# Low-rank tiles 5.2 apart instead of 4.4, their three products in another order, and the last block inversion spread over 32 instead of 25

## The chip, the cores and the metric

The kernel runs on one core of one Trainium2 chip. The metric is the device time of one execution in microseconds, and of several executions the median. The engines are named as in the profile: PE multiplies matrices (PEld is its loading of the stationary operand), DVE, ACT and POOL work elementwise, SP issues most of the DMAs.

## The reference, cut to what matters

Two layers on 512 positions of width 2048. Layer 0 is forgetting attention, layer 1 is RWKV-7 time mixing; each is a gated branch with a residual add. The change lies in layer 1:

```python
xx = jnp.pad(h[:, :-1], ((0, 0), (1, 0), (0, 0))) - h
xr, xw, xk, xv, xa, xg = (h + xx * mu[i] for i in range(6))
r, k, v, z = xr @ w_in[0], xk @ w_in[1], xv @ w_in[2], xg @ w_in[3]
w_log = -softplus(-(w0 + tanh(xw @ w1) @ w2)) - 0.5
v = v + (v_first - v) * sigmoid(v0 + (xv @ v1) @ v2)
a = sigmoid(a0 + (xa @ a1) @ a2)
# per head, over 512 steps: S = S * w_t + (S a_t) b_t + v_t k_t ; y_t = S r_t
```

The first factors of the low-rank pairs, w1 (96 columns), a1 (96) and v1 (64), are the *low-rank stage* here. The recurrence is done in chunks of 64 steps, and each chunk needs the inverse of a unit triangular 64x64 matrix per head; the 32x32 diagonal blocks of four 128-row tiles (eight heads) are inverted together, so there are four *block inversions*.

## The kernel before, in words

Positions lie along the free axis (512), the width in 16 tiles of 128 partitions. A product of full precision is made of three matmuls of rounded halves: high by high, low by high, high by low (`mm3`). The *backbone* is the chain of the large projections: 16 output tiles per weight, each of 16 input tiles, so 48 matmuls into a bank named `pj`. In layer 1 it goes through 10 tiles of k, then 16 each of r, v, z and the output. Its weights come by SP (`raw`), are rounded by ACT (`whi`), and DVE makes the rest (`wlo`), once for every four input tiles, that is once for 12 `pj` matmuls.

All else runs beside the backbone as tasks. A planner (`Flow`) keeps a clock that only the issued matmuls advance: a matmul of 512 columns counts 0.213. A task yields numbers, each the time on that clock after which it goes on. PE, DVE and ACT take their instructions strictly in the order in which the planner issued them, so a changed number changes these orders, from its place to the end of the program.

- `lora_k(q, k)` is the low-rank stage for input tile k. It loads the hidden tile (`hp`) and the weights (`rawl`); POOL makes the difference `d` to the position before; DVE makes three mixed operands `m` (for w, a and v, in this order); ACT rounds each (`mh`); the rests (`ml`) are made by POOL for w and by DVE for a and v; DVE also makes the rest of the weights, `wll`. Then three products, each three matmuls, go into banks: w and a into two named `S`, v into `y`. `side` starts one such tile every 4.4.
- `keys` prepares the operands of four 128-row tiles and then starts `invert` for them. A block inversion is 30 steps of two operations on `lane` and `lt`, by POOL for the first three groups and by DVE for the last (`DG = (3,)`), with a yield after each step. `inverse` takes the result further with small matmuls (`x<-t,gab` and `x<-qt,us`), started for the last group at `DINV + 8`:

```python
e = dve if grp in DG else pool
e.tensor_tensor(out=t, in0=m[:, 0:s, s:s + 1]..., in1=m[:, s:s + 1, s + 1:]..., op=OP.mult)
e.tensor_tensor(out=m[:, 0:s, s + 1:], in0=m[:, 0:s, s + 1:], in1=t, op=OP.add)
if grp in DG:
    yield DINV / 30
```

- `mixing` brings the 16 input tiles of the next projection: loads (`hp`), `hi` by ACT, `lo` by DVE or POOL, in a burst at the end of the projection before. `values` finishes v (loads `sv` and `vf`, three DVE operations per tile). The recurrence (`recur`) starts when all inverses are there and ends before the output projection begins.

Of the kernel before, what the change touches and what calls it, by code (L numbers as in the profile page):

```python
# [131 lines left out]
def body(ctx, tc, a, out, dbg=None, stop=0):  # L132
# [26 lines left out]
    def bank(tag, bufs=None):  # L159
        return cur["p"].tile([P, T], F, tag=tag, bufs=cur["t"][tag], name=tag)  # L160
# [71 lines left out]
    def act_hi(hi, src):  # L232
        act.activation(hi, src, AF.Copy)
# [19 lines left out]
    def mm3(o, w, k, x, first, last, m0=0, m1=P):  # L253
        wh, wl = w
        xh, xl = x
        pe.matmul(o, wh[:, k, m0:m1], xh, start=first, stop=False)
        pe.matmul(o, wl[:, k, m0:m1], xh, start=False, stop=False)
        pe.matmul(o, wh[:, k, m0:m1], xl, start=False, stop=last)
# [30 lines left out]
    def silu_c(mp):  # L289
        cb = mp.tile([P, D], F, name="cb", bufs=1)  # L290
        cs = mp.tile([P, KT], F, name="cs", bufs=1)
        i = act.activation(cs, vecs[:, V_C], AF.Silu)
        return cb, cs, i
# [17 lines left out]
    def load(q, src, tag, shape=(P, T), bufs=None):  # L311
        t = q.tile(list(shape), F, tag=tag, name=tag, bufs=bufs)
        sp.dma_start(t, src)
        return t
# [81 lines left out]
    with ExitStack() as s0:  # L396
# [7 lines left out]
        with tc.tile_pool(name="st0", bufs=2, reuse_waits="tile") as q:  # L404
# [97 lines left out]
            cb, cs, i = silu_c(cbp)  # L502
# [11 lines left out]
            for i in range(4):  # L514
                o = bank("tr")
# [619 lines left out]
    def keep(j, o):  # L1135
        t = mq.tile([P, T], F, tag="z", name="kt")
        act.activation(t, o, AF.Copy)
        yield 1.5
        sp.dma_start(kTd[j], t)


    lspan = ((0, LW), (LW, LW + LA_), (NL - P, NL))
    lb, la = [], []

    def lora_k(q, k):
        if k == 0:
            lb.extend(bank(t) for t in "SSy")
        hp = load(mq, h1d[k], "hp", (P, T + 1), bufs=NHP)
        raw = load(q, a["lora"][k], "rawl", (P, NL))
        yield 4  # L1150
        wh = q.tile([P, 1, NL], R, tag="whl", name="whl")
        wl = q.tile([P, 1, NL], R, tag="wll", name="wll")
        act_hi(wh[:, 0], raw)
        ns = (1, 4, 3)
        ms = [q.tile([P, T], F, tag=f"m{n}", name="m", bufs=1 + (n == 3)) for n in ns]
        d = q.tile([P, T], F, tag="d", name="d")
        pool.tensor_tensor(out=d, in0=hp[:, 0:T], in1=hp[:, 1:], op=OP.subtract)
        ts = [tuple(q.tile([P, T], R, tag=f"m{x}{n}", name="m" + x) for x in "hl") for n in ns]
        yield 1.4
        for i in range(5):  # L1160
            if i == 1:
                dve.tensor_tensor(out=wl[:, 0], in0=raw, in1=wh[:, 0], op=OP.subtract)
            if i < 3:
                dve.scalar_tensor_tensor(out=ms[i], in0=d,
                                         scalar=vecs[:, V_MU + ns[i], k:k + 1],
                                         in1=hp[:, 1:], op0=OP.mult, op1=OP.add)
            if 1 <= i < 4:
                act_hi(ts[i - 1][0], ms[i - 1])
            if 2 <= i:
                e = pool if i - 2 < 1 else dve  # L1170
                e.tensor_tensor(out=ts[i - 2][1], in0=ms[i - 2], in1=ts[i - 2][0],
                                op=OP.subtract)
            yield 0.7
        yield 1
        sp.dma_start(mxd[0, k], ms[2])
        premixed.add((0, k))
        for t, o, (m0, m1) in zip(ts, lb, lspan):
            mm3(o[0:m1 - m0, :], (wh, wl), 0, t, k == 0, k == KT - 1, m0, m1)
            yield 1
        if k == KT - 1:  # L1180
            lb.append(None)

    def lora_act(q):
        for o, (m0, m1), fn, nm in zip(lb, lspan, (AF.Tanh, AF.Copy), "wa"):
            t = q.tile([m1 - m0, T], F, tag="t", name="t", bufs=1)
            act.activation(t, o[0:m1 - m0], fn)
            h = q.tile([m1 - m0, T], R, tag=nm + "h", name=nm + "h", bufs=1)
            l = q.tile([m1 - m0, T], R, tag=nm + "l", name=nm + "l", bufs=1)
            split(h, l, t)
            la.append((h, l))  # L1190
        t = q.tile([2 * LV, T], F, tag="t", name="t", bufs=1)
        o = lb[2][P - LV:]
        for i in range(2):
            act.activation(t[i * LV:i * LV + LV], o, AF.Copy)
        h = q.tile([2 * LV, T], R, tag="vh", name="vh", bufs=1)
        l = q.tile([2 * LV, T], R, tag="vl", name="vl", bufs=1)
        pool.memset(l[LV:].bitcast(F), 0.0)
        act_hi(h, t)
        dve.tensor_tensor(out=l[0:LV], in0=t[0:LV], in1=h[0:LV], op=OP.subtract)
        la.append((h, l))  # L1200
# [3 lines left out]
    def lora_w(q, g, n):  # L1204
        nm, rows = (("w2", LW), ("a2", LA_), ("v2", LV))[n]
        raw = load(q, a[nm][:, g * T:(g + 1) * T], "w2r", (rows, T), bufs=3)
        if n == 2:
            wh = q.tile([2 * LV, T], R, tag="v2h", name="v2h", bufs=2)
        else:
            wh = q.tile([rows, T], R, tag="w2h", name="w2h", bufs=4)  # L1210
            wl = q.tile([rows, T], R, tag="w2l", name="w2l", bufs=4)
        yield 6.5
        act_hi(wh[0:rows], raw)
        yield 1.2
        if n == 2:
            dve.tensor_tensor(out=wh[LV:], in0=raw, in1=wh[0:LV], op=OP.subtract)
        else:
            dve.tensor_tensor(out=wl, in0=raw, in1=wh, op=OP.subtract)
        yield 1.2
        uw[g, n] = (wh,) if n == 2 else (wh, wl)  # L1220
# [529 lines left out]


    STW = 5
    DG, DINV = (3,), 25
    HOP = 3.9
    INV, KEY = 54, 9.8

    def side(q):
        for j, o in enumerate(ks):
            fl.start(0, keep(j, o))
        for k in range(KT):  # L1760
            fl.start(fl.t, lora_k(q, k))
            yield 4.4
        while len(lb) < 4:
            yield 0.2
        yield 0.5
        pools.close()
        q = pools.enter_context(tc.tile_pool(name="uq", bufs=2, reuse_waits="tile"))
        for n in range(3):
            fl.start(fl.t, lora_w(q, 0, n))
        rmask = q.tile([P, NCH, C], F, name="rmask", bufs=1)  # L1770
        pool.memset(rmask, 1.0)
        pool.memset(rmask[:, :, 0:1], 0.0)
        rms.append(rmask)
        lora_act(q)
        yield 3.5
        for j in range(KT):
            for n in range(3):
                if j % 4 == 0 and j < KT - 4:
                    fl.start(fl.t, lora_w(q, j // 4 + 1, n))
                fl.start(fl.t, lora_up(q, j, n))  # L1780
                yield 0.8
        while len(ups) < 3 * KT:
            yield 0.2
        yield 3
        pools.close()
        kp = pools.enter_context(tc.tile_pool(name="kp", bufs=1, reuse_waits="tile"))
        eIs.append(kp.tile([P, NCH, C + 1], F, name="eI"))
        for i in range(5):
            qts.append(kp.tile([P, NCH, C], F, name=f"qt{i}"))
            for r in (32, 96):  # L1790
                pool.memset(qts[i][r:r + 32, :, 0:32], 0.0)
        pool.memset(eIs[0][:, :, 0:1], 1.0)
        for j in range(KT):
            if "v" in dbg:
                print("keys", j, fl.t, len(ends))
            fl.start(fl.t, keys(kp, j))
            fl.start(fl.t + 5, mixz(kp, j))
            yield KEY
        while len(qd) < KT or len(premixed) < 3 * KT:
            yield 0.2  # L1800
        yield 3
        pools.close()
        rk = pools.enter_context(tc.tile_pool(name="rk", bufs=1, reuse_waits="tile"))
        for i in range(4):
            QP.append([rk.tile([P, NJ, C], F, name=f"QP{i}{h}") for h in range(2)])
            GP.append([rk.tile([P, NJ, C], F, name=f"GP{i}{h}") for h in range(2)])
            for h in range(2):
                pool.memset(QP[i][h][OS[h]], 0.0)
                pool.memset(GP[i][h][OS[h]], 0.0)
        def stages():  # L1810
            for n in range(NG * NU):
                g, u = divmod(n, NU)
                while any(NJ * g + i not in rd for i in range(NJ)):
                    yield 0.2
                yield from stage(rk, g, u)

        fl.start(fl.t, stages())
        fl.start(fl.t, recur(rk))

    fl.start(0, side(q))  # L1820
    Av, Ar, Az, G = [], [], [], []
    ready = {(id(A), k) for k in range(KT)}
# [37 lines left out]
```

## Time and profile before

| what | us |
|---|---|
| runs of the kernel before | 2422.9, 2425.7, 2427.42; median 2425.7 |
| profiled execution, its own time | 2421.53 |
| its span, first to last instruction | 2419.5 |
| PE busy in the span | 2307.1 |
| PE not busy in the span | 112.4 |

The rows below come from the profiled execution; microseconds count from the start of its span. All rows have the line of one helper (L90), so the names of the tiles tell the place. The granted clock is given as a share of 2.4 GHz.

### The profile page before, as it was taken

Reading aid. Unit: us, or ns where it says so; the run is one execution under the profiler, and the core shown is the slowest. Engines: PE = TensorE matmul, PEld = TensorE weight load, DVE = VectorE, ACT = ScalarE, POOL = GpSimd, SP = SyncE. Lnnn points to the kernel's source line nnn. Section 1 sums busy time; section 2 is a strip of 40 time slices with the busy share of each in tenths; the row PEclk is TensorE's granted clock in tenths of the full one; section 3 lists DMA queues with packets and bytes.
Section 4 is the critical chain, followed back from the end, with each engine's and each line's share of the span. In section 5 each row is a group of like instructions: output and inputs, shape, how many; then the busy total and the mean of one; then the engine's idle time right before and its main releaser. Section 6 shows DMA issues by size and latency. Waiting matters only on the chain. (4 is left out here: it accounts for less than half of the span.)

```text
span 2419.5 us, 39366 instructions
## 1 busy us (share of the span) xinstructions
PE 2307.1 (95%) x13626; PEld 1804.9 (75%) x13626; DVE 1611.3 (67%) x2850; ACT 1254.4 (52%) x2298; POOL 699.6 (29%) x1114
## 2 busy tenths in 40 slices
PE   6999899999999999998999999889899989999999
PEld 4787677877777778886766767667677767777887
DVE  6886678788888645336797667666577777655322
ACT  3436655555555544225646777754345556665221
POOL 0003333434333110110141209851264545440000
PEclk8999999999999999999999999999999999999999
DMA  8864366666666365445756999877776766645543
GB/s 310 323 226 157 112 202 210 216 215 221 209 220 207 123 199 189 144 135 153 224 168 212 296 282 274 262 213 200 217 198 180 200 183 192 179 121 173 160 138 96
DMA packets 388151, 480.22 MB, mean 198 GB/s; under 512 B 146032, under 2 KB 217840, under 8 KB 384112
## 3 DMA queue, kind: packets, MB, share of 16 engines
q1 hardware_dynamic: 386288, 475.08, 63.3%
q0 software_dynamic: 1664, 2.63, 0.3%
q8 instruction: 108, 1.77, 0.3%
q14 instruction: 91, 0.75, 0.1%
HBM read 381.63 MB, written 95.95 MB: 197 GB/s over the span
## 5 line engine op out<-in xcount | busy, mean ns | idle before, releaser
L90 PE MATMUL pj<-hi,whi 128*128 128x512 f32 x2416 | 985.7, 408 | 14.6 <-ACT hi L90 8.2
L90 PE MATMUL pj<-hi,wlo 128*128 128x512 f32 x2416 | 958.0, 397 | 6.1 <-DVE wlo L90 6.1
L90 PE MATMUL pj<-lo,whi 128*128 128x512 f32 x2416 | 958.7, 397 | 0.0
L90 DVE TENSOR_TENSOR wlo<-raw,whi 128x512 fp32r<-128x512 f32 (+2 forms) x628 | 477.8, 768 | 278.5 <-ACT whi L90 275.2
L90 ACT ACTIVATE whi<-raw 128x512 fp32r<-128x512 f32 (+2 forms) x628 | 394.1, 634 | 423.7 <-PE pj L90 221.2
L90 PEld LDWEIGHTS pj<-hi,whi 128*128 128x128 f32 x2416 | 458.7, 190 | 119.7 <-ACT hi L90 9.0
L90 PEld LDWEIGHTS pj<-lo,whi 128*128 128x128 f32 x2416 | 457.4, 189 | 108.7 <-DVE lo L90 0.2
L90 PEld LDWEIGHTS pj<-hi,wlo 128*128 128x128 f32 x2416 | 459.0, 190 | 100.0 <-DVE wlo L90 7.4
L90 DVE CUSTOM_DVE_ANT_0 wm<-wm,cb 128x1024 f32<-128x1024 f32 x128 | 156.6, 1224 | 0.3
L90 POOL TENSOR_SCALAR SV<-SV,dec 64x64 f32<-64x64 f32 x224 | 98.8, 463 | 108.6 <-DVE SV L90 71.6
L90 ACT ACTIVATE pr<-Sm,mx 128x128 f32<-128x128 f32 (+3 forms) x128 | 71.5, 558 | 85.5 <-POOL mx L90 81.5
L90 POOL TENSOR_SCALAR mx<-mx 128x1 f32<-128x1 f32 x128 | 65.6, 513 | 154.9 <-DVE mx L90 117.9
L90 POOL TENSOR_SCALAR pr<-pr,rc 128x128 f32<-128x128 f32 (+3 forms) x128 | 87.6, 685 | 33.0 <-DVE rc L90 29.6
L90 DVE CUSTOM_DVE_ANT_0 Sm<-S,cmask 128x128 f32<-128x128 f32 (+3 forms) x128 | 62.0, 485 | 36.0 <-PE S L90 35.4
L90 POOL TENSOR_TENSOR lt<-lane 128x30 f32<-128x30 f32 (+14 forms) x90 | 63.2, 702 | 64.0 <-DMA lane<-mld 57.1
L90 POOL TENSOR_TENSOR lane<-lane,lt 128x30 f32<-128x30 f32 (+14 forms) x90 | 65.6, 729 | 7.1
L90 POOL TENSOR_TENSOR bk<-bk,eI 128x512 f32<-128x512 f32 x32 | 36.5, 1140 | 105.0 <-PE S L90 59.6
L90 PE MATMUL S<-k,q 128*128 128x128 f32 (+7 forms) x256 | 62.6, 327 | 0.0
L90 POOL TENSOR_TENSOR acc<-acc,sq 128x512 f32<-128x512 f32 x14 | 18.1, 1295 | 150.8 <-ACT sq L90 150.8
L90 PE MATMUL tr<-ident,pr 128*128 128x128 f32 x320 | 57.3, 277 | 4.3 <-DVE pT L90 1.4
L90 PEld LDWEIGHTS tr<-ident,pr 128*128 128x128 f32 x320 | 41.6, 141 | 25.4 <-ACT pT L90 6.9
L90 DVE SCALAR_TENSOR_TENSOR hp<-pj,gate,hp 128x512 f32<-128x512 f32 x16 | 12.0, 751 | 68.9 <-PE pj L90 68.9
(325 smaller groups left out, 3282.4 us busy)
## 6 DMA issues: line engine op xcount, KB each, us to landing
wm<-in_wmodT SPq DMA_DIRECT2D x132, 512.0 KB, 4.4
raw<-in_wz SPq DMA_DIRECT2D x128, 256.0 KB, 3.8
raw<-in_wo SPq DMA_DIRECT2D x128, 256.0 KB, 3.5
raw<-in_wv SPq DMA_DIRECT2D x124, 256.0 KB, 3.9
wm<-in_wmodT SPq DMA_DIRECT2D x30, 1024.0 KB, 6.8
raw<-in_wk SPq DMA_DIRECT2D x96, 256.0 KB, 3.7
raw<-in_wr SPq DMA_DIRECT2D x64, 256.0 KB, 4.8
raw<-in_wq SPq DMA_DIRECT2D x56, 256.0 KB, 3.6
```

The costliest lines, as they stand in the source:

```text
L90: self.last = f(*a, **k)
```

## The change

The start of the next low-rank tile is 5.2 of the planner's clock away, not 4.4. The three products of a tile are issued as a, v, w instead of w, a, v, so that the one whose rest comes from POOL is last. The last block inversion spreads its 30 steps over 32 of the clock, not 25; as its `inverse` tasks start at `DINV + 8`, they are 7 later too.

```diff
-        for t, o, (m0, m1) in zip(ts, lb, lspan):
+        for t, o, (m0, m1) in ((ts[i], lb[i], lspan[i]) for i in (1, 2, 0)):
             mm3(o[0:m1 - m0, :], (wh, wl), 0, t, k == 0, k == KT - 1, m0, m1)
             yield 1
...
-    DG, DINV = (3,), 25
+    DG, DINV = (3,), 32
...
         for k in range(KT):
             fl.start(fl.t, lora_k(q, k))
-            yield 4.4
+            yield 5.2
```

On PE, in the low-rank stage, one tile before: its rows (`S_11402` is the bank of w, `S_11403` of a, `y` of v; `ml` is the rest that DVE or POOL made) stand like this, and the next tile's w follows after 6 or 9 more `pj` rows.

```order
L90 MATMUL S_11402<-mh_11747,whl_11739 96x512
L90 MATMUL S_11402<-mh_11747,wll_11740 96x512
L90 MATMUL S_11402<-ml_11748,whl_11739 96x512
L90 MATMUL pj_11733<-hi_10939,whi_11652 128x512
L90 MATMUL pj_11733<-hi_10939,wlo_11653 128x512
L90 MATMUL pj_11733<-lo_10940,whi_11652 128x512
L90 MATMUL S_11403<-mh_11749,whl_11739 96x512
L90 MATMUL S_11403<-mh_11749,wll_11740 96x512
L90 MATMUL S_11403<-ml_11750,whl_11739 96x512
```

On PE at the same place in the changed program: a comes first (its last row stands on top here), then v, then w, and the next tile's a follows after 9 or 15 `pj` rows.

```order
L90 MATMUL S_11403<-ml_11781,whl_11770 96x512
L90 MATMUL pj_11699<-hi_11233,whi_11725 128x512
L90 MATMUL pj_11699<-hi_11233,wlo_11726 128x512
L90 MATMUL pj_11699<-lo_11234,whi_11725 128x512
L90 MATMUL y_11404<-mh_11782,whl_11770 128x512
L90 MATMUL y_11404<-mh_11782,wll_11771 128x512
L90 MATMUL y_11404<-ml_11783,whl_11770 128x512
L90 MATMUL pj_11699<-hi_11275,whi_11725 128x512
L90 MATMUL pj_11699<-hi_11275,wlo_11726 128x512
L90 MATMUL pj_11699<-lo_11276,whi_11725 128x512
L90 MATMUL S_11402<-mh_11778,whl_11770 96x512
```

From the first tile's first product to the last tile's, 201 `pj` rows stood before and 261 stand now; the stage's own matmuls are the same, and everything on PE behind the stage comes 57 `pj` rows later against the backbone (the first matmul of the recurrence 48, its last 57).

On DVE, in the last block inversion, before (steps of two rows on `lane` and `lt`; `wlo` belongs to the backbone):

```order
L90 TENSOR_TENSOR wlo<-raw,whi 128x512
L90 TENSOR_TENSOR lt<-lane 128x130
L90 TENSOR_TENSOR lane<-lane,lt 128x5x26
L90 TENSOR_TENSOR lt<-lane 128x150
L90 TENSOR_TENSOR lane<-lane,lt 128x6x25
L90 TENSOR_TENSOR lt<-lane 128x168
L90 TENSOR_TENSOR lane<-lane,lt 128x7x24
L90 TENSOR_TENSOR wlo<-raw,whi 128x512
```

And the same steps on DVE in the changed program (`lo<-hp,hi` belongs to the mixing burst):

```order
L90 TENSOR_TENSOR wlo<-raw,whi 128x512
L90 TENSOR_TENSOR lt<-lane 128x130
L90 TENSOR_TENSOR lane<-lane,lt 128x5x26
L90 TENSOR_TENSOR lt<-lane 128x150
L90 TENSOR_TENSOR lane<-lane,lt 128x6x25
L90 TENSOR_TENSOR lo<-hp,hi 128x512
L90 TENSOR_TENSOR wlo<-raw,whi 128x512
L90 TENSOR_TENSOR lt<-lane 128x168
L90 TENSOR_TENSOR lane<-lane,lt 128x7x24
L90 TENSOR_TENSOR wlo<-raw,whi 128x512
```

Between the first and the last row of the inversion stood 10 `wlo`, 5 `lo` and 4 transposes of `inverse`; now 12, 8 and 4.

## Rows read from the trace of the kernel before

**Rows 1.** Page, part 1: busy time, share of the span, instructions of each engine.

```profile
PE 2307.1 (95%) x13626; PEld 1804.9 (75%) x13626; DVE 1611.3 (67%) x2850; ACT 1254.4 (52%) x2298; POOL 699.6 (29%) x1114
```

**Rows 2.** Windows: a dense stretch, low-rank stage, last inversion, recurrence, stretch behind it.

```profile
core 0: us, PE busy (x) PEld busy (x) DVE busy (x) ACT busy (x) POOL busy (x), PEclk, DMA share, GB/s
1020.00:1080.00 60.00, 60.00 (x260) 48.62 (x259) 23.10 (x29) 17.01 (x29) 7.76 (x6) 1.00 0.42 140
1201.50:1294.50 93.00, 85.23 (x343) 59.08 (x342) 90.99 (x111) 45.27 (x85) 43.19 (x32) 1.00 0.52 165
1610.20:1646.50 36.30, 28.89 (x167) 22.40 (x167) 34.59 (x80) 13.75 (x24) 7.89 (x6) 0.91 0.66 193
1740.00:2168.00 428.00, 409.13 (x4079) 321.26 (x4080) 308.27 (x652) 243.15 (x423) 211.45 (x385) 0.99 0.66 179
2168.00:2240.00 72.00, 72.00 (x428) 57.24 (x427) 36.78 (x71) 37.05 (x59) 1.96 (x6) 1.00 0.56 173
```

**Rows 3.** Instructions that write or read ml, whole trace: duration ns min/median/max, first and last start.

```profile
L90 DVE TENSOR_TENSOR ml<-m,mh x32: 677/680/1352, 1201.7 to 1294.3; 128x512 fp32r<-128x512 f32 x32
L90 POOL TENSOR_TENSOR ml<-m,mh x16: 1296/1403/1997, 1198.7 to 1290.9; 128x512 fp32r<-128x512 f32 x16
L90 PE MATMUL y<-ml,whl x16: 391/430/504, 1204.5 to 1295.6; 128*128 128x512 f32 x16
```

**Rows 4.** The same for hp: two rows.

```profile
L90 DVE SCALAR_TENSOR_TENSOR m<-d,vecs,hp x48: 736/740/1779, 1190.1 to 1292.8; 128x512 f32<-128x512 f32 x48
...
L90 POOL TENSOR_TENSOR d<-hp x16: 1094/1370/1497, 1176.1 to 1282.1; 128x512 f32<-128x512 f32 x16
```

**Rows 5.** Groups, 1201.5 to 1294.5: busy us, mean ns, idle before.

```profile
L90 DVE SCALAR_TENSOR_TENSOR m<-d,vecs,hp 128x512 f32<-128x512 f32 x46 | 41.9, 918 | 0.0
...
L90 DVE TENSOR_TENSOR ml<-m,mh 128x512 fp32r<-128x512 f32 x32 | 28.6, 892 | 2.0 <-ACT mh L90 1.9
...
L90 POOL TENSOR_TENSOR ml<-m,mh 128x512 fp32r<-128x512 f32 x15 | 22.8, 1519 | 36.3 <-ACT mh L90 34.3 <-DMA mxd<-m 2.0
L90 DVE TENSOR_TENSOR wlo<-raw,whi 128x512 fp32r<-128x512 f32 x18 | 22.4, 1247 | 0.0
L90 POOL TENSOR_TENSOR d<-hp 128x512 f32<-128x512 f32 x14 | 19.3, 1378 | 13.9 <-PE S L90 12.2 <-DMA raw<-in_wk 1.7
...
L90 DVE TENSOR_TENSOR wll<-rawl,whl 128x256 fp32r<-128x256 f32 x15 | 6.2, 413 | 0.0
```

**Rows 6.** Waits, 1201.5 to 1294.5: us in total, times, longest.

```profile
PEld S L90 <- POOL ml L90: 12.5, 14, 1.5
...
PEld S L90 <- DVE ml L90: 4.4, 7, 0.7
PEld y L90 <- DVE ml L90: 2.7, 8, 0.6
```

**Rows 7.** Timeline of one low-rank tile: start, duration, engine, instruction.

```profile
1205.81 1.98 POOL L90 TENSOR_TENSOR ml<-m,mh 128x512 fp32r<-128x512 f32 x1 [2.56 <-ACT mh L90]
...
1206.59 1.75 DVE L90 SCALAR_TENSOR_TENSOR m<-d,vecs,hp 128x512 f32<-128x512 f32 x1
...
1207.84 0.16 PEld L90 LDWEIGHTS S<-ml,whl 128*96 128x96 f32 x1 [1.50 <-POOL ml L90]
...
1208.26 2.13 DVE L90 TENSOR_TENSOR ml<-m,mh 128x512 fp32r<-128x512 f32 x2
...
1208.47 1.37 POOL L90 TENSOR_TENSOR d<-hp 128x512 f32<-128x512 f32 x1 [0.68 <-PE S L90]
```

**Rows 8.** Waits, 1604 to 1650.

```profile
DVE lt L90 <- DMA lane<-mld: 9.7, 1, 9.7
...
PE pj L90 <- DVE wlo L90: 6.1, 3, 3.7
```

**Rows 9.** Groups on DVE, 1610.2 to 1646.5.

```profile
L90 DVE TENSOR_TENSOR lt<-lane 128x30 f32<-128x30 f32 (+14 forms) x30 | 13.0, 433 | 10.3 <-DMA lane<-mld 9.7
L90 DVE TENSOR_TENSOR lane<-lane,lt 128x30 f32<-128x30 f32 (+14 forms) x30 | 11.9, 397 | 1.0
L90 DVE TENSOR_TENSOR wlo<-raw,whi 128x512 fp32r<-128x512 f32 x11 | 7.5, 683 | 0.0
L90 DVE TENSOR_TENSOR lo<-hp,hi 128x512 fp32r<-128x512 f32 x5 | 3.4, 682 | 0.0
L90 DVE STREAM_TRANSPOSE t<-qt 32x256 f32<-32x256 f32 x4 | 1.7, 430 | 0.1
```

## The prediction

> **What bounds the kernel now.** I read the page's busy times first. PE is busy for 2307.1 of 2419.5 us [rows 1], and its work is the same before and after, so the change can only act on the 112.4 us in which PE stands, and on stretches at a lower clock. The windows come next. In a dense stretch 260 matmuls take 60.0 us, that is 0.2308 us each [rows 2]; the reader may use this as the price of any 512-column matmul. The low-rank stage, 1201.5 to 1294.5, holds 343 of them, which is 79.2 us of work in 93.0 us: some 13.8 us are lost, although the row calls PE busy for 85.23 (a waiting matmul's record is longer). In the same row DVE is busy for 90.99 of 93.0 us, 98%, at full clock and half DMA load. DVE, not PE, sets the pace there. POOL and PE tell the same in the waits: PEld waits 12.5 us for POOL's rest, but also 4.4 and 2.7 us for DVE's rests [rows 6], and POOL in turn stands 34.3 us waiting for ACT, which rounds what DVE made [rows 5].
>
> The timeline of one tile shows how [rows 7]. POOL's ml runs 1205.81 to 1207.79; DVE's third m, begun at 1206.59, takes 1.75 us where its median is 0.740 [rows 4]; then two ml take 2.13 us for a median of 0.680 each [rows 3]. PE meanwhile holds for POOL's ml until 1207.84. A DVE operation is lengthened when a POOL operation runs.
>
> One tile takes 6.07 us: the v product's rows run from 1204.5 to 1295.6 over 15 steps, 91.1 us [rows 3].
>
> **The spacing, 4.4 to 5.2.** The stage held 201 backbone matmuls between its first and last product, now 261: per tile 13.4, now 17.4, plus 9 of its own. PE needs 22.4 x 0.2308 = 5.17 us per tile before and 26.4 x 0.2308 = 6.09 after. The 60 matmuls moved in are 13.85 us of work that need not be done later. What the stage lengthens by is to be subtracted. DVE is busy 98% of 6.07, 5.94 us per tile. Per tile it gets 4/12 of a wlo more, at 0.683 us [rows 9] 0.23, so 6.17 us. PE's 6.09 and DVE's 6.17 are nearly equal; with the 0.13 that DVE stood per tile before, I take 6.30 us. Fifteen steps are then 94.5 us, 3.4 more than before, and the stage gives 13.85 - 3.4 = **10.5 us**. Bounds: if DVE's lengthening shrinks as DVE finds gaps, PE's 6.09 sets the pace, 91.4 us, and the gain is 13.6. If the added wlo costs the 1.247 us that it costs in this stage [rows 5], a tile takes 5.94 + 0.42 + 0.13 = 6.49, and the gain is 7.6.
>
> **The order a, v, w.** POOL's rest is now needed after six backbone matmuls and the six of two products, 12 x 0.2308 = 2.8 us after the first slot; its longest wait was 1.5 us [rows 6], so that wait goes. Late next is a: in the timeline DVE's first ml ends at 1208.26 + 0.68 = 1208.94, 1.15 us after POOL's. If DVE keeps pace, PE pays these 1.15 us once, when the stage begins, and is then in phase; if it doesn't, the wait is part of DVE's 6.30 already. I put 0 beside the 0.13 per tile kept above (2.0 in the stage). The DMAs of each tile (hp, rawl, mxd) are the same in number; on SP they now stand among more weight loads, and the five first loads of the next mixing still alternate with the last low-rank loads. POOL's order of d and ml is unchanged. I price this at nothing: DMAs are busy 52% there [rows 2]. Without that cover a late hp would hold one tile's d, 1.4 us [rows 4].
>
> **The inversion, 25 to 32.** From 1610.2 to 1646.5 DVE is busy 34.59 of 36.3 us, PE 28.89, and the granted clock is 0.91 on average, a part of it at 1.2 GHz [rows 2]. PE waits 6.1 us for wlo, once 3.7 [rows 8]. DVE's work there is 13.0 + 11.9 on the inversion, 10 wlo, 5 lo and 4 transposes, 6.8 + 3.4 + 1.7 [rows 9]: 36.8 us. After, with 12 wlo and 8 lo (0.682), it is 24.9 + 8.2 + 5.5 + 1.7 = 40.3, 3.5 more. But the two wlo stand for 24 backbone matmuls, 5.5 us of PE work. DVE's excess falls by **2.0 us**, which I take. Bounds: all of the 6.1 and of the low clock's 9% of 36.3, 3.3 us, goes (9.4), or nothing does, since DVE also stands 9.7 us for the lane load ahead of the first step [rows 8], which stays. The seven later starts of inverse cost nothing as long as the recurrence's first matmuls, 48 backbone rows later, still come behind them; they do in the order.
>
> **What lies behind.** Keys, inversions and recurrence keep their neighbours nearly, but the backbone is some 57 matmuls, 13.2 us, further on beside them. PE stands 18.9 us in the recurrence's window [rows 2], and such waits will be dealt anew: 0, with 5 us either way. At the end PE has no idle from 2168 to 2240 (72.0 of 72.0), so the recurrence's end has room there.
>
> The sum against the profiled execution's own time is 2421.53 - 10.5 - 2.0 = 2409.0 us. The median of the runs shown is 4.2 us above that execution, so the median comes to 2425.7 - 12.5 = **2413.2 us**. Its own range is 2407 to 2420, from 13.6 and 7.6 for the stage and 5 us for the waits behind.
>
> **A rule that speaks against it.** DVE's and POOL's operations overlap only in part: in rows 7 POOL's d goes its normal 1.37 us beside two ml of which the second is lengthened. By the Trainium skill, "SBUF — State Buffer", section "Who interferes with whom", a DVE instruction with two SBUF inputs and a POOL instruction that reads SBUF exclude each other for a whole instruction. The trace agrees that one is held, but not for all of the other's length. By the rule alone the time would be that of the second rival below, 2437 us in place of 2413.
>
> **Rivals.**
> - *The loss stays under another name.* DVE falls behind again, and PE waits for a's rest instead of POOL's. For it: the 1.15 us, and DVE at 98%. If a tile takes 6.79 us, 0.62 above DVE's 6.17, the stage lengthens by 10.8 and gives 3.0; with nothing from the inversion 2422.7 us. Against it: nothing is added on DVE but a third of a wlo per tile.
> - *POOL and DVE exclude each other fully* (slower). Place: the low-rank stage. DVE's undisturbed work per tile is 3 x 0.740 + 2 x 0.680 + 0.413 + 17.4/12 x 0.683 = 4.98 us [rows 3 to 5, 9], POOL's 1.403 + 1.370 = 2.77 [rows 3, 4]: 7.75 us per tile, 116.3 for the stage, 25.2 more for 13.85 of work, 2425.7 + 11.3 = 2437 us. It decides from 6.99 us per tile on, where the lengthening eats the 13.85; slower by more than 0.2% from 7.3 on. Against it: the same count before, with 13.4/12 wlo, gives 7.53, and a tile took 6.07.
> - *The inversion collides with more.* It now holds 8 lo instead of 5 and comes nearer to the tasks of v. A wait like that of 3.7 us with half clock behind it, 3.3 us, costs 7.0. Four of them, less the 9.4 there now, are 18.6 us more, 2425.7 - 10.5 + 18.6 = 2434 us; up to two change little, and three end near 2427.
> - *More than the sum.* The stage at PE's pace (13.6) and the whole 9.4 of the inversion: 2402.7 us.
>
> **How the numbers follow.** About 0.2%, 4.9 us, is what a measurement of this kernel can tell from no change. The forecast has 0.63, the first rival 0.17 (no change), full exclusion 0.04 and the collision 0.07 (slower), more than the sum 0.09. Faster is 0.63 + 0.09 = 0.72, the same 0.17, slower 0.11. The range reaches from 2404 to 2427: it takes in the forecast and the first rival, and leaves out the slower cases and most of the last.
>
> **What would show it.** Right: v's products from first to last in 93 to 96 us; PEld's wait for POOL's ml near zero; DVE still over 95% in the stage; PE's wait for wlo in the inversion under 6 us; PE standing some 100 us in the whole span. Wrong: PEld waiting over 10 us for DVE's ml of a (first rival); POOL's ml longer than 1.5 us with tiles above 7 us (second); new waits for wlo near the inversion (third); or the stage's gain there and new waits in the recurrence of over 5 us.

## The result and the profile after

The changed kernel takes 2414.36 us (median of 6 executions, 2409.21 to 2417.79) where the kernel before took 2425.34 beside it (6 executions, 2422.9 to 2427.53): a ratio of 0.9949, with a 95% interval of 0.9938 to 0.996 (the two medians by themselves stand at 0.9955). By the medians it is faster by 11.0 us; 12.5 were forecast.

The profiled execution took 2413.1 us, 8.4 less than that of before. The profile of before lay 4 us under its median and that of after 1.3 us, so the profiles can explain 8.4 of the 11.0 us; where other executions of before lose the rest is not in them. The changed kernel's page, part 1 (as [rows 1]), shows the same work on PE, which now stands for 103.2 us of a span of 2411.2 where it stood for 112.4:

```profile
PE 2308.0 (96%) x13626; PEld 1807.8 (75%) x13626; DVE 1605.5 (67%) x2850; ACT 1257.2 (52%) x2300; POOL 686.2 (28%) x1114
```

Its windows, with the columns of [rows 2]: the low-rank stage and the last inversion.

```profile
1202.50:1299.70 97.20, 94.74 (x399) 71.49 (x400) 95.09 (x116) 48.42 (x91) 42.72 (x32) 1.00 0.57 179
1616.50:1658.50 42.00, 35.19 (x246) 26.68 (x245) 39.83 (x84) 17.86 (x34) 10.46 (x8) 0.88 0.64 190
```

Its instructions on ml (as [rows 3]), and below them who waited for any of these (us in total, times):

```profile
L90 DVE TENSOR_TENSOR ml<-m,mh x32: 676/686/1523, 1202.5 to 1298.1; 128x512 fp32r<-128x512 f32 x32
L90 POOL TENSOR_TENSOR ml<-m,mh x16: 1288/1410/2015, 1199.5 to 1295.0; 128x512 fp32r<-128x512 f32 x16
L90 PE MATMUL y<-ml,whl x16: 391/393/502, 1205.2 to 1299.7; 128*128 128x512 f32 x16
...
  PEld S L90: 5.5, 8
...
  PEld y L90: 1.3, 3
```

The products of v run from 1205.2 to 1299.7, 94.5 us, 6.30 per tile. The stage now takes in 399 matmuls, 92.1 us of work at 0.2308 each, in 97.2 us: 5.1 are lost, where 13.8 were. PEld's waits for POOL's ml [rows 6] are gone, and 6.8 us of waits for DVE's ml are left. DVE is still busy for 95.09 of 97.2 us, 6.16 per tile.

For the rest of the program I add up PE's losses by section: for every two successive matmuls in the trace, what the time between their starts exceeds the dense time of the first (0.232 us at 512 columns) by, if that is over 0.03 us. The sections are bounded by the first and last matmuls of the stages named. This sum is worked out and is no view of the profile; it leaves out what a lower clock takes if it is spread over many matmuls only a little. In the keys and the recurrence many matmuls are short, and their dense time is an assumption; so there only the differences between kernels are read, and these to about 1 us.

| PE's loss, us | before | after |
|---|---|---|
| up to the first v product | 90.9 | 92.5 |
| low-rank stage, first to last v product | 13.9 | 4.6 |
| second factors of the low-rank pairs | 6.7 | 6.9 |
| keys | 42.5 | 43.6 |
| last inversion, to the recurrence's first matmul | 15.0 | 15.8 |
| recurrence | 73.6 | 68.2 |
| behind the recurrence | 0.2 | 4.2 |

The rows add up to 7.0 us less, of the 8.3 by which the span is shorter. The 1.6 us more up to the first v product arise in the first 100 us, where the two programs are the same, so they are not the change's. The stage gives 9.3 us and the recurrence 5.4. The inversion section gives nothing on balance, and behind the recurrence, where no time was lost before, there are 4.2 us of new loss. Those are waits of PE and PEld for wlo in the waits of the changed kernel from 2203 to 2242:

```profile
DVE z L90 <- DMA yp<-ypd: 7.6, 3, 4.2
DVE lo L90 <- ACT hi L90: 6.7, 3, 3.5
ACT hi L90 <- DMA hp<-gd: 6.4, 3, 3.9
PEld pj L90 <- DVE wlo L90: 4.7, 4, 1.8
...
PE pj L90 <- DVE wlo L90: 3.0, 4, 1.4
```

The timeline of the changed kernel at 2227 shows why PE waits for wlo although ACT's half of that weight was ready. DVE takes its instructions in order; ahead of the wlo stands a lo of the mixing burst, which waits for a DMA (hp<-gd) by way of ACT's hi:

```profile
2227.61 1.28 ACT L90 ACTIVATE hi<-hp 128x512 fp32r<-128x512 f32 x2 [3.93 <-DMA hp<-gd]
2228.27 0.69 DVE L90 TENSOR_TENSOR lo<-hp,hi 128x512 fp32r<-128x512 f32 x1 [3.52 <-ACT hi L90]
...
2228.88 0.68 DVE L90 TENSOR_TENSOR wlo<-raw,whi 128x512 fp32r<-128x512 f32 x1
...
2229.61 0.19 PEld L90 LDWEIGHTS pj<-hi,wlo 128*128 128x128 f32 x1 [1.80 <-DVE wlo L90]
```

In words: the output projection's last inputs depend on the recurrence's result, which now comes 57 backbone matmuls later against the backbone.

### The profile page after: what moved, and what is told of

It reads as the page before. It is cut to its first block, busy times and chain, and to the rows that moved or that the text cites. A ratio compares the mean times of both kernels' runs of the same rounds, so it can differ in the third digit from the quotient of the medians.

```text
span 2411.2 us, 39377 instructions
## 1 busy us (share of the span) xinstructions
PE 2308.0 (96%) x13626; PEld 1807.8 (75%) x13626; DVE 1605.5 (67%) x2850; ACT 1257.2 (52%) x2300; POOL 686.2 (28%) x1114
## 5 line engine op out<-in xcount | busy, mean ns | idle before, releaser
L90 PE MATMUL pj<-hi,whi 128*128 128x512 f32 x2416 | 987.5, 409 | 14.2 <-ACT hi L90 8.2
L90 POOL TENSOR_SCALAR SV<-SV,dec 64x64 f32<-64x64 f32 x224 | 93.4, 439 | 105.9 <-DVE SV L90 71.7
```

The lines of the kernel that those rows point to most:

```text
L90: self.last = f(*a, **k)
```

## The experiments

The theory at the start: DVE, kept busy by its own work and lengthened by POOL's operations, sets the low-rank stage's pace; the spacing fills that stage with backbone matmuls, the order only names the operand that PE waits for, and the inversion's spreading pays where PE waits for wlo. The rivals: the order is what removed the loss; or the gain lies in waits behind that were only dealt anew. The kernel before gave medians of 2423.05 to 2426.08 us beside the runs below, so runs of different series are compared by their ratios to it.

### One part alone

*e1_order* has only the order a, v, w.

```diff
-        for t, o, (m0, m1) in zip(ts, lb, lspan):
+        for t, o, (m0, m1) in ((ts[i], lb[i], lspan[i]) for i in (1, 2, 0)):
```

> The order a, v, w alone, at 4.4 and 25. First theory, DVE sets the low-rank stage's pace: its work per tile is unchanged, so the v products from first to last still take some 91 us (90 to 93), PE's wait moves from POOL's rest to DVE's rests, and the time is 2425 within 5 us. Rival, POOL's late rest is a loss of its own: its 12.5 us of PEld waits go without another in their place, the stage takes some 80 us and the time is near 2414.

2427.37 us against 2426.08, ratio 1.0008 (0.9995 to 1.0021): nothing. The stage takes 91.3 us and loses 14.8. The waits of this kernel from 1200 to 1311 show the loss under the name that my first rival gave it, PEld waiting for DVE's rest in place of POOL's; 15.5 + 5.3 us here answer to 12.5 + 4.4 + 2.7 in [rows 6]:

```profile
PEld S L90 <- DVE ml L90: 15.5, 16, 1.4
PE S L90 <- DVE ml L90: 7.7, 12, 0.9
PEld y L90 <- DVE ml L90: 5.3, 14, 0.9
```

*e2_space* has only the spacing.

```diff
-            yield 4.4
+            yield 5.2
```

> The spacing 5.2 alone, order w, a, v and 25. DVE sets the pace: the stage takes 93 to 96 us with 60 more backbone matmuls in it, and the time is near 2415 (2410 to 2420); PEld's wait for POOL's rest falls from 12.5 to under 4 us by the spacing alone. Rival, POOL's late rest is a loss of its own: PE still waits some 0.8 us per tile for it, the stage takes some 103 us, and the time is near 2424.

2419.14 against 2426.08, ratio 0.9971 (0.996 to 0.9981), about 7 us. The stage takes 95.7 us and loses 5.6, with PEld still waiting 4.5 us for POOL's ml (waits of this kernel from 1200 to 1311). Behind it this kernel loses 5.4 us more than before in the inversion section and 4.3 more behind the recurrence, so the time is 4 us above the middle of what was expected.

```profile
PEld S L90 <- POOL ml L90: 4.5, 4, 2.1
```

*e3_inv* has only the inversion over 32.

```diff
-    DG, DINV = (3,), 25
+    DG, DINV = (3,), 32
```

> The inversion over 32 alone, spacing 4.4 and the old order. By the forecast's term PE's waits for wlo near the inversion fall from 6.1 to some 4 us and the time is near 2423. Rival, DVE has no more room in that stretch than before: the waits for wlo stay at 5 to 8 us and the time is 2425 within 4 us.

2416.25 against 2426.08, ratio 0.9962 (0.9947 to 0.9977): 9.8 us, nearly as much as all three parts together, where some 3 were expected. Near the inversion (waits of this kernel from 1600 to 1703) PE waits 2.0 us for wlo where it waited 6.1 [rows 8], and some 4 us for other things on `x`:

```profile
PE x L90 <- DVE t L90: 3.8, 3, 1.8
...
PE pj L90 <- DVE wlo L90: 2.0, 2, 1.7
```

The inversion section loses 2.5 us less than before, the recurrence 3.8 less. Its profiled span is 5.4 us shorter; the rest of the 9.8 is again the distance between the profile of before and its median.

*e4_space_order* is the changed kernel with the inversion over 25.

```diff
-    DG, DINV = (3,), 32
+    DG, DINV = (3,), 25
```

> Spacing 5.2 and the order a, v, w, the inversion over 25: the whole change without its last part. By the forecast it lacks the inversion's 2 us: some 2416. Rival, the inversion's spread gave nothing: 2414 or less. The low-rank stage is that of the changed kernel in either case, 93 to 96 us.

2420.56 against 2426.08, ratio 0.9979 (0.9968 to 0.9991). The stage takes 94.5 us and loses 4.6, so the order is worth 1.0 us of it once the spacing is there, but the whole is no faster than with the spacing alone, and 4.6 us above what was expected. PE's waits for wlo near the inversion (1600 to 1703) are 8.2 us, first row below, and 6.1 in the changed kernel, second row:

```profile
PE pj L90 <- DVE wlo L90: 8.2, 4, 3.5
```

```profile
PE pj L90 <- DVE wlo L90: 6.1, 4, 1.7
```

*f4_order_inv* has the order and the inversion over 32 at the old spacing, both edits as above.

> The kernel before with the order a v w and the inversion over 32, tiles 4.4 apart as before. The order alone gave 2427.4 against 2426.1, the inversion alone 2416.2. If the order is worth nothing without the spacing: 2415-2419, stage 91 us. If parts simply add: 2417.5. If the order is worth more once the inversion is spread: under 2413.

2416.86 against 2423.05, ratio 0.9982 (0.9973 to 0.9992), stage 91.4 us. The time fell where the first case put it, but against the kernel before it gained 6 us, less than the inversion alone, with intervals that overlap. At the old spacing the order is worth nothing or costs a little.

### What sets the low-rank stage's pace

*e5_no_wll* takes one DVE operation per tile away: the product reads the rounded weights twice, so the rests of the first factors' weights are left out of the result.

```diff
-        wl = q.tile([P, 1, NL], R, tag="wll", name="wll")
...
-            if i == 1:
-                dve.tensor_tensor(out=wl[:, 0], in0=raw, in1=wh[:, 0], op=OP.subtract)
...
-            mm3(o[0:m1 - m0, :], (wh, wl), 0, t, k == 0, k == KT - 1, m0, m1)
+            mm3(o[0:m1 - m0, :], (wh, wh), 0, t, k == 0, k == KT - 1, m0, m1)
```

> The kernel before without DVE's operation that makes the rest of the low-rank weights (wll); its matmuls stay and take the high half twice. One look. DVE sets the pace: each tile is shorter by that operation's 0.41 us, the v products from first to last take some 85 us instead of 91 (83 to 87). Rival, POOL's late rest alone sets it: the stage stays at 90 to 92 us.

One execution, 2417.43 us against 2424.23. The products of v run over 85.8 us, 5.3 less; 15 of the operations of 0.413 us [rows 5] are 6.2. PE's work in the stage is the same, so what became shorter is DVE's.

*e6_no_d* takes the POOL operation that reads away: d is a constant, so the shift by one position is left out of the result.

```diff
-        pool.tensor_tensor(out=d, in0=hp[:, 0:T], in1=hp[:, 1:], op=OP.subtract)
+        pool.memset(d, 0.5)
```

> The kernel before with POOL's difference d replaced by a POOL memset of the same tile, which reads nothing: the shift to the position before is left out of the low-rank operands. One look. If POOL's reading operations lengthen DVE's (0.5 to 0.6 us for each of two per tile), DVE's m, ml and wlo come nearer to 0.74, 0.68 and 0.68 us on average and the stage takes 81 to 86 us. Rival, DVE's long operations have another cause: their means stay at 0.92, 0.89 and 1.25 us and the stage at 90 to 92 us.

One execution, 2416.14 against 2424.23. The products of v run over 82.1 us, 9.0 less, with nothing taken from DVE or PE. The instructions on ml of this kernel show that DVE's ml is not lengthened once; its mean in the stage was 892 ns [rows 5]:

```profile
L90 DVE TENSOR_TENSOR ml<-m,mh x32: 675/682/694, 1204.2 to 1287.7; 128x512 fp32r<-128x512 f32 x32
L90 POOL TENSOR_TENSOR ml<-m,mh x16: 1295/1408/2012, 1201.2 to 1284.3; 128x512 fp32r<-128x512 f32 x16
```

9.0 us over 15 tiles is 0.60 us of DVE for each d of 1.37 us on POOL. DVE is busy for 82.14 of 84.0 us in this shorter stage (1201 to 1285), so it still sets the pace.

*f1_d_early_44* keeps the whole computation, the old spacing and order and the inversion over 32, and lets POOL make d one section earlier.

```diff
+    dfd = dr.tile([KT, P, T], F, name="dfd")
...
+                df = q.tile([P, T], F, tag="df", name="df")
+                pool.tensor_tensor(out=df, in0=hp[:, 0:T], in1=hp[:, 1:], op=OP.subtract)
+                sp.dma_start(dfd[k], df)
...
+        d = load(q, dfd[k], "d")
...
-        d = q.tile([P, T], F, tag="d", name="d")
-        pool.tensor_tensor(out=d, in0=hp[:, 0:T], in1=hp[:, 1:], op=OP.subtract)
...
-    DG, DINV = (3,), 25
+    DG, DINV = (3,), 32
```

> Tiles 4.4 apart, the old order, the inversion over 32, and POOL's difference d made in the section before (the positions' mixing of the residual stage, PE dense there) and brought back by a DMA of 256 KB per tile; everything is still computed. Beside it: the inversion alone, 2416.2. If DVE's lengthening by POOL's operations is what sets the low-rank stage's pace, 16 operations of POOL fewer in it bring the stage near the 82.1 us that it took with a memset in d's place, 9 us less than before, and the time to 2405-2411. Rival: the loss only moves, since d meets DVE in the section before, or the added 4 MB out and 4 MB in delay other loads: 2414-2424, with PE waiting before 1200 us or for hp and raw.

2413.04 against 2423.05, ratio 0.996 (0.9945 to 0.9976), which is what the inversion gives alone; the time lies between the two cases that were expected. The products of v run over 81.3 us and the stage loses 4.0, as the theory had it; but the loss up to the stage rises by 11.6 us, some 9 of them in the section with df, as the rival had it. Groups on DVE and POOL in the section ahead, first of this kernel (1112 to 1200), then of the kernel before (1112 to 1190); the columns are those of [rows 5]:

```profile
L90 DVE SCALAR_TENSOR_TENSOR m<-hp,vecs,g 128x512 f32<-128x512 f32 x16 | 21.4, 1337 | 1.6 <-ACT g L90 1.6
L90 POOL TENSOR_TENSOR df<-hp 128x512 f32<-128x512 f32 x16 | 18.8, 1173 | 60.2 <-ACT hp L90 48.4 <-issue 11.7
...
L90 DVE SCALAR_TENSOR_TENSOR mr<-hp,vecs,mr 128x512 f32<-128x512 f32 x16 | 12.8, 797 | 0.0
L90 DVE SCALAR_TENSOR_TENSOR xn<-x,scale,rs 128x512 f32<-128x512 f32 x16 | 12.6, 790 | 0.0
```

```profile
L90 DVE SCALAR_TENSOR_TENSOR mr<-hp,vecs,mr 128x512 f32<-128x512 f32 x16 | 11.9, 746 | 0.0
L90 DVE SCALAR_TENSOR_TENSOR xn<-x,scale,rs 128x512 f32<-128x512 f32 x16 | 11.9, 744 | 0.0
L90 DVE SCALAR_TENSOR_TENSOR m<-hp,vecs,g 128x512 f32<-128x512 f32 x16 | 11.9, 744 | 1.6 <-ACT g L90 1.6
```

The three DVE groups grow by 9.5 + 0.9 + 0.7 = 11.1 us, 0.69 for each df. The price of a d is about the same in either section. Not all of PE's loss here is DVE's: 3.5 us are one wait for ACT's kt, ahead of which ACT stands 5.4 us for a weight load (in the kernel before it stands 5.1 for the same load, and PE does not come to wait). That the rest is paid in PE's time here too suggests that DVE is near its limit in this section as well (74.0 of 88 us busy); no run shows that by itself.

*f2_d_early_52* is the changed kernel with d made earlier in the same way.

> The changed kernel whole (5.2, order a v w, 32) with d made in the section before. Its stage loses only 4.6 us against dense matmuls, so there is little left to take: the stage goes from 94.5 to 90-92 us, and the time from 2414.4 to 2409-2414. If spacing and d do the same thing, this ends above the run at 4.4 with d early, because the 4 us of waits behind the recurrence, which come with 5.2, stay. Rival: they add up, and the time falls by 9 us to 2403-2407.

2414.46 against 2423.05, ratio 0.9961 (0.9947 to 0.9974). The v products take 90.5 us and the stage loses nothing any more; ahead of it 6.3 us more are lost than in the changed kernel, and behind the recurrence 3.8 stay. The spacing and the earlier d remove the same loss and do not add up.

### Other doses

*e7_space60* and *e8_space48* are the changed kernel with another spacing.

```diff
-            yield 5.2
+            yield 6.0
```

> The changed kernel with a spacing of 6.0 instead of 5.2 (321 backbone matmuls in the stage, not 261). First theory: PE now sets the stage's pace, 21.4 backbone and 9 own matmuls per tile, 7.02 us, 105 to 107 us in all, its waits for rests fall below 3 us; but the recurrence ends some 11 us later against the output projection, and the waits before that projection grow from 4 to 10 to 17 us: time 2418 to 2426. Rival, there is room at the end: those waits stay below 6 us and the time is 2410 to 2414.

2447.78 against 2424.23, ratio 1.0093 (1.0076 to 1.0109): I missed this one by over 20 us. The stage does lose only 0.7 now, but the losses come back, in us more than in the changed kernel, 11.5 from the last v product to the last of the second factors, 10.2 in the inversion section, 8.3 in the recurrence and 13.7 behind it. This last is nearly one wait, in the waits of this kernel from 2195 to 2300, for ACT, which releases the bank:

```profile
PE pj L90 <- ACT z L90: 14.9, 1, 14.9
```

```diff
-            yield 5.2
+            yield 4.8
```

> The changed kernel with a spacing of 4.8 (234 backbone matmuls in the stage). DVE sets the pace: 15.6 backbone matmuls per tile, DVE 6.07 + 0.13 us, the stage takes 92 to 94 us and PE loses some 9 us in it, half-way between 13.9 and 4.6; the waits before the output projection are 1 to 2 us. Sum: some 2414 (2411 to 2417), about the changed kernel. Rival, what the spacing gives in the stage is its whole worth: 2418 or more.

2431.59 against 2424.23, ratio 1.0026 (1.0016 to 1.0036): missed as well. The stage loses 9.9, between 4.6 and 13.9 as it should, but the keys lose 48.4 (42.5 before), the recurrence 75.4 and the end 3.5. Both doses give the stage what the theory says and lose it elsewhere, and more.

*f3_inv40* is the kernel before with the inversion over 40.

```diff
-    DG, DINV = (3,), 25
+    DG, DINV = (3,), 40
```

> The kernel before with the last inversion over 40 in place of 25 (32 alone gave 2416.2, 9.1 us less than before, of which PE's waits for wlo at the inversion fell from 6.1 to 2.0 us and the recurrence's waits by some 4 us). If the spreading pays by DVE's excess over PE in the inversion, only 2.0 us are left: 2414-2417. If a good part of the 9.1 was a lucky deal of the recurrence's waits, this one deals them anew: up to 2419-2426, although the waits for wlo stay under 3 us. If the later inverse comes to hold the recurrence's start, PE's first waits in the recurrence show it, and the time goes above 2420 too.

2422.53 against 2423.05, ratio 0.9995 (0.9984 to 1.0006): what 32 gains, 40 loses again, as the second case had it. The inversion section loses 3.2 us less than before and even less than at 32, with 1.4 us of waits for wlo. The recurrence begins 33 backbone rows later than at 32 and loses 80.5 us, 10.7 more than there, the largest new wait being PE's for POOL's dec (PE's waits of this kernel from 1729 to 2204.7):

```profile
PE S L90 <- DVE vf L90: 6.8, 4, 3.0
PE S L90 <- POOL dec L90: 6.2, 1, 6.2
PE S L90 <- ACT GP L90: 5.0, 3, 2.4
```

### The losses of all of them side by side

From the trace of each, in us, added up as above, but with the inversion only to its own last matmul (0.4 to 0.5 us less than to the recurrence's first). The room is the time from the recurrence's last matmul to the first of the output projection, whose inputs the recurrence's results become; the last row counts the matmuls between the two.

| | before | e1 | e3 | f1 | f4 | f3 | e8 | e2 | e4 | after | f2 | e7 |
|---|---|---|---|---|---|---|---|---|---|---|---|---|
| low-rank stage | 13.9 | 14.8 | 14.2 | 4.0 | 15.0 | 13.7 | 9.9 | 5.6 | 4.6 | 4.6 | 0.0 | 0.7 |
| keys | 42.5 | 41.9 | 43.3 | 39.8 | 40.5 | 41.3 | 48.4 | 43.4 | 43.8 | 43.6 | 42.4 | 35.7 |
| last inversion | 14.5 | 17.0 | 12.0 | 12.1 | 11.9 | 11.3 | 17.6 | 19.9 | 18.0 | 15.4 | 16.5 | 25.6 |
| recurrence | 73.6 | 75.7 | 69.8 | 68.6 | 69.1 | 80.5 | 75.4 | 73.5 | 73.5 | 68.2 | 67.5 | 76.5 |
| behind it | 0.2 | 0.2 | 0.2 | 0.2 | 0.2 | 2.3 | 3.5 | 4.5 | 5.4 | 4.2 | 3.8 | 17.9 |
| room | 43.8 | 43.8 | 43.8 | 43.8 | 43.8 | 36.4 | 36.9 | 31.5 | 32.1 | 31.6 | 31.3 | 28.8 |
| matmuls in it | 187 | 187 | 187 | 187 | 187 | 148 | 148 | 130 | 130 | 130 | 130 | 58 |

The last three rows are read together. A wait ahead of the projection's first matmul lengthens the room itself: e7's 28.8 us hold only 58 matmuls, 13.4 us of work, and its long wait. So the matmuls are the measure: with 187 nothing is lost behind the recurrence, with 148 it is 2.3 to 3.5, with 130 3.8 to 5.4, with 58 17.9. The loss goes with the room, whether the spacing or a later inversion takes it.

## Why the prediction was right, step by step

**DVE sets the stage's pace: shown.** Taking 0.413 us of DVE's work per tile away (e5) and taking a POOL operation away that lengthens DVE's (e6) both shorten the stage with PE's work unchanged; e5 and e6 are single executions, but f1, four executions with the whole computation, shortens it as e6 does. The rival that the order removed the loss falls with e1.

**The spacing, 10.5 us: right, and nearly in its size.** The products of v were forecast at 94.5 us and took 94.5; DVE's busy time per tile was forecast at 6.17 us and is 6.16. Of the two prices for an added wlo, 0.683 and 1.247, the lower holds: from 4.4 over 4.8 to 5.2 the stage's DVE busy time goes 90.99, 92.95, 95.09 us with 18, 21 and 24 wlo, some 0.68 each. These are DVE's groups in the changed kernel's stage, 1202.5 to 1299.7, with the columns of [rows 5]:

```profile
L90 DVE SCALAR_TENSOR_TENSOR m<-d,vecs,hp 128x512 f32<-128x512 f32 x45 | 44.8, 1016 | 0.0
...
L90 DVE TENSOR_TENSOR ml<-m,mh 128x512 fp32r<-128x512 f32 x32 | 29.5, 932 | 1.8 <-ACT mh L90 1.6
...
L90 DVE TENSOR_TENSOR wlo<-raw,whi 128x512 fp32r<-128x512 f32 x24 | 21.3, 887 | 0.0
```

The mean duration of wlo falls from 1247 to 887 ns while m rises from 918 to 1016 and ml from 892 to 932: POOL lengthens whichever operation it meets, and more operations do not make more of it. The loss in the stage fell by 9.3 and not by 10.5. Most of the difference is a count: from the stage's first product to its last matmul stood 204 `pj` rows, not 201, and now stand 261, so 57 were added and not 60, 13.2 us of work; less the 3.4 that is 9.8.

**The order, 0: right, and now with the reason.** Alone it renames the wait (e1). With the spacing the stage loses 4.6 in place of 5.6, but e2 and e4 differ by less than their intervals.

**The inversion, 2.0 us: the mechanism was right where I placed it, the sum lacked the larger half.** From e4 to the changed kernel the waits for wlo fall by 2.1 us and the section's loss by 2.6, as reckoned. But the times differ by 6.2 us (2420.56 to 2414.36, each with its own comparison: 0.9979 and 0.9949), and most of this is the recurrence, 73.5 to 68.2. Alone (e3) it is the same: 2.5 in the section and 3.8 in the recurrence. In the kernel before the clock granted in the inversion was 0.91 and now it is 0.88, so of the upper bound of 9.4 the part that was the low clock's did not come. Against the kernel before the section gives nothing, because the spacing had made it worse (e2, e4); PE's waits for wlo are 6.1 us there as before, so of the signs named for a right forecast this one, under 6 us, just failed to come, while the other four came.

**What lies behind, 0 with 5 us either way: right in sum and wrong in one reason.** I wrote that PE has no idle from 2168 to 2240 and that "the recurrence's end has room there". It had, but a stretch in which PE does not stand does not tell how much: 57 matmuls less of it (13.2 us) cost 3.6 to 5.2 us. The inversion section lost 3.5 to 5.4 more with the spacing (e2, e4). In the changed kernel 4.0 of the one and 0.9 of the other are left, and the recurrence's 5.4 pays for them. So the sum came out near the forecast with terms in it that I did not have, and that they cancel is luck. The 5 us either way were too narrow as well: with the same account of the stage, e8 came out some 17 us and e7 over 20 us above what was expected.

**The rivals.** The loss under another name appears in e1 and not in the change. The slow case of full exclusion did not come: its 7.75 us per tile stand against 6.30 measured. By the Trainium skill, "SBUF — State Buffer", section "Who interferes with whom", a DVE operation with two inputs in SBUF contends with a POOL operation that reads SBUF, and what they contend for is an exclusive lock. e6 and f1 agree with it: a memset on POOL lengthens nothing, a subtraction does, and by the rows of the last section DVE's operation waits until POOL's is done. So the two do exclude each other, and it was my sum that was wrong, and with it the 7.53 by which I spoke against the rule. Three things in it cost DVE nothing. The records of successive DVE operations overlap, by 7.1 us between the first and the last v product of the kernel before, 0.47 per tile. POOL's 1.403 and 1.370 hold waiting already, and the 1.37 that I called normal for a d is not; undisturbed its ml takes 1.29 us and a d 1.04, as the shortest in the changed kernel show:

```profile
L90 POOL TENSOR_TENSOR d<-hp x16: 1041/1369/1556, 1177.9 to 1285.7; 128x512 f32<-128x512 f32 x16
```

And a part of the waiting falls on POOL, which has time to spare. Added up in the trace of before, DVE's operations last 1.61 us per tile longer than undisturbed ones, and POOL's means [rows 5] lie 0.23 and 0.34 above the shortest: 2.18 us in all, of the 2.33 that POOL's two operations take. With d gone (e6, f1) DVE's 1.61 become 1.08. The collision in the inversion did not come: its longest wait for wlo is 1.7 us after 3.7.

**Left open.** Why the recurrence loses some 4 to 5 us less in five kernels with the inversion over 32 (e3, f1, f2, f4 and the changed one: 67.5 to 69.8; the kernels with 25, e5 and e6 among them: 73.2 to 75.7), while at 40 it loses 10.7 more than in e3. e7 and e8 have 32 too and lose 76.5 and 75.4, so the 32 alone does not decide it. In the kernel before PE waits twice for ACT's vt there, 6.1 us; in e3 once, 3.8, and in the changed kernel not at all, but it waits 8.3 us for GP where it waited 3.7. These are PE's waits from 1720 to 2206, first of the kernel before, then of the changed one:

```profile
PE S L90 <- ACT vt L90: 6.1, 2, 3.3
PE S L90 <- ACT GP L90: 3.7, 5, 1.4
```

```profile
PE S L90 <- ACT GP L90: 8.3, 5, 4.1
PE S L90 <- ACT mhi L90: 3.9, 1, 3.9
PE S L90 <- DVE mlo L90: 1.8, 4, 0.6
```

I can say that the orders of the engines meet differently there, not by what rule. No run moved the recurrence alone, so more than a third of what the change gains before its new losses (5.4 us beside the stage's 9.3) has no cause shown.

## What to carry to other kernels

Where a secondary engine is full, the stage's price is that engine's busy time per unit of work, and one can fill PE's idle time there with other matmuls; which operand PE waits for last said nothing here. Work that is moved up in a program with fixed orders on each engine changes every later meeting: look at the distance between the last producer and the stage that consumes it (here 187 matmuls, 43.8 us, of which 39 could not be spared without loss), not at whether PE is busy in between. And one good dose doesn't make a trend: with the order a, v, w and 32, the spacings 4.4 (f4), 4.8, 5.2 and 6.0 lost 15.0, 9.9, 4.6 and 0.7 us in the stage they act on, and the ratios to before were 0.9982, 1.0026, 0.9949 and 1.0093, as the waits behind were dealt anew.

## What the runs showed of the hardware that was not expected

Where an operation of POOL and one of DVE meet that both read two tiles, one of the two keeps its duration, or nearly, and the other waits until it is done; it can be either. The timeline of f1 in the section ahead of the stage, where they meet in the same way at twelve of the sixteen tiles:

```profile
1139.92 0.74 DVE L90 SCALAR_TENSOR_TENSOR mr<-hp,vecs,mr 128x512 f32<-128x512 f32 x1
1140.38 1.19 POOL L90 TENSOR_TENSOR df<-hp 128x512 f32<-128x512 f32 x1 [3.28 <-issue]
1140.59 1.53 DVE L90 SCALAR_TENSOR_TENSOR m<-hp,vecs,g 128x512 f32<-128x512 f32 x1
```

df takes 1.19 us, 0.15 more than the 1.04 that it takes where it meets nothing, since the mr is still running when it starts; and DVE's m waits. df ends at 1141.57, and m, whose normal duration is 0.74, at 1142.12, 0.55 us later. The other way round, in the low-rank stage of the same kernel:

```profile
1216.04 2.01 POOL L90 TENSOR_TENSOR ml<-m,mh 128x512 fp32r<-128x512 f32 x1 [4.94 <-ACT mh L90]
1216.21 0.68 DVE L90 TENSOR_TENSOR wlo<-raw,whi 128x512 fp32r<-128x512 f32 x1
...
1216.82 1.78 DVE L90 SCALAR_TENSOR_TENSOR m<-d,vecs,hp 128x512 f32<-128x512 f32 x1
```

Here the wlo goes at its normal 0.68 us and POOL's ml takes 2.01 where its shortest is 1.29, 0.72 more, about one wlo; then m waits for ml, which ends at 1218.05, and ends 0.55 us behind it at 1218.60, as above.

The 0.55 us are no accident of these rows. In the traces of all the kernels here I took each d, df and ml of POOL in the stage and the section ahead of it (1100 to 1305) that ends while a DVE operation with two inputs, begun over 0.1 us before, is still running. That operation then ends 0.54 to 0.56 us later in all 405 cases with 512 columns, 0.28 later in all 13 with 256 (wll), and 0.81 to 0.82 later in all 11 with 768 (wlo in the section ahead). What is left to do grows with the columns, 1.07 ns for each, and undisturbed operations of 256, 512 and 768 columns take 0.41, 0.68 and 0.94 us, that is the same and some 0.13 more. So DVE had done none of its columns before POOL was finished: the two take turns by whole operations, and only the fixed 0.13 to 0.19 us of a DVE operation lie beside POOL's. What decides whose turn it is these rows don't show: at 1216 the wlo goes first, and in other tiles of the same run a wlo that starts just as long after POOL's ml waits for it.
